# Tying the second block's preparation on VectorE to the place in the FFN where it was emitted

## The chip, the cores and the metric

The kernel runs on one core of a Trainium2 chip. The metric is the device time of one execution in microseconds. The kernel before takes 1735.87 us (median of 3 runs, 1732.74 to 1736.22).

## What is computed

A sequence of 512 tokens of width 1024 goes through two blocks. Block 1 is a gated delta rule beside a dilated attention, and then an FFN with a short convolution on its gate:

```python
h = rmsnorm(x, ln2[l])
gate = causal_dwconv(h @ w_gate[l], ffn_conv[l])
x = x + (jax.nn.silu(gate) * (h @ w_up[l])) @ w_down[l]
```

Block 2 mixes an SSM (`s5_mixer`) with a sparse attention and ends in a mixture of experts; an `ada` vector modulates it. Part of block 2 depends on weights alone. For the SSM that is the powers of each state's complex decay, the discretised input matrix, and tables of their products with the output matrix:

```python
mag = jnp.exp(lr * dt)
ab_re, ab_im = mag * jnp.cos(li * dt), mag * jnp.sin(li * dt)
bb_re = cr[..., None] * br - cim[..., None] * bim
```

For `ada` it is the product of a small vector `c` with a weight matrix of 1024 by 6144. This weight-only work is called the preparation here. The FFN's width is 2816, which is 22 column chunks of 128.

## The kernel before

`body` builds block 1, then hands the preparation to a `Filler` and calls `ffn`. The preparation is two generators run side by side by `both`, `ssm_prep` and `ada`; each `yield` ends a piece. `ffn` asks for pieces with `F.tick`: one before each gate load and one before each up load of a pair of chunks, two before each down load, and `F.finish()` for the rest in the last group.

`ffn` works in three groups of 8, 8 and 6 chunks. In a group, `K.ws` (L171 to L173) computes gate and up for a pair of chunks, c and c+1, in 48 matmuls each. `act` (L1013 to L1025) applies the convolution, the activation and the split into a high and a low part (`ahi`, `alo`). Then the down product (L1051 to L1053) runs in two halves of the output, n=0 and n=1, each over four weight tiles u=0, 2, 4, 6 of 24 matmuls. Every 128x1024 weight tile is loaded by SyncE (L143), rounded to `whi` on ScalarE (L153), and its remainder `wlo` is taken on VectorE (L154). TensorE uses a tile as three products, the third (second in the down product) with `wlo`. `wraw`, `whi` and `wlo` have three buffers each, the PSUM accumulators `mm` a ring of four.

The preparation's own parts that the text speaks of: on VectorE the `ada` accumulations L1117 and L1119, two of them after each load of an `araw` tile (L1111, two buffers) and 96 in all; chains of small 128x16 to 128x64 operations (L1204 to L1245), five doublings of a cosine and sine table (L1275 to L1280), and `bb` (L1317 to L1322). On GpSimd `pmul` (L1350 to L1352) builds V1 from `bb` in 48 operations, then the 16 tiles `s5v` (two buffers), which SyncE stores to `V3d` (L1368). `crow` are four loads (L1333) that TensorE transposes (L1335).

A tile scheduler orders each engine's instructions: it knows of data and buffers, not of the pieces' places. Nothing ties an instruction of a piece to the tick that emitted it, so it may be put ahead of FFN instructions that were emitted before it. An engine then runs its list in order.

Of the kernel before, what the change touches and what calls it, by code (L numbers as in the profile page):

```python
# [9 lines left out]
F32 = mybir.dt.float32  # L10
# [55 lines left out]
def both(a, b):  # L66
    for _ in zip_longest(a, b):
        yield


class Filler:


    def __init__(self):
        self.q = []

    def add(self, *gens):
        self.q.extend(gens)
# [1 line left out]
    def tick(self, n=1):  # L80
        while n and self.q:
            try:
                next(self.q[0])
                n -= 1
            except StopIteration:
                self.q.pop(0)
# [7 lines left out]
class Core:  # L94
# [54 lines left out]
    def split(self, raw, m=1024, eng=None, pool=None, bufs=3):  # L149

        nc = self.nc
        hi, lo = ((pool or self.w).tile([128, 1024], F32R, name=n, tag=n, bufs=bufs) for n in ("whi", "wlo"))
        nc.scalar.copy(hi[:, :m], raw[:, :m])  # L153
        (eng or nc.vector).tensor_sub(lo[:, :m], raw[:, :m], hi[:, :m].bitcast(F32))  # L154
        return hi, lo

    def ws(self, src, c0, n, xhi, xlo, nk, width=T):
# [202 lines left out]
def block1_mix(K):  # L360
# [3 lines left out]
    w_in = i["w_in"][0]  # L364
    F = Filler()
    left, right = ExitStack(), ExitStack()
# [32 lines left out]
    gst = ExitStack()  # L399
    G = Gdn(K, gst, F, w_in, hhi, hlo)  # L400
    G.first(wt)
# [9 lines left out]
    qk = S.qk_proj(0)  # L411
    F.add(qk)
    G.scan(yhi[0], ylo[0])
# [32 lines left out]

    F.finish(qk)
    S.attend(sst, F, out_half(0, False), yhi[1], ylo[1])
    F.add(out_half(1, True))
    F.finish()  # L450
# [525 lines left out]
def ffn(K, x, ss, F, last):  # L976


    nc, tc, i = K.nc, K.tc, K.i
    wg, wu, wd = i["w_gate"][0], i["w_up"][0], i["w_down"][0]  # L980
    with ExitStack() as st:
        P = lambda *a, **k: st.enter_context(K.pool(*a, **k))
        hp = P(name="fh", bufs=1)
        hhi = hp.tile([128, 8, T], F32R, name="hhi")
        hlo = hp.tile([128, 8, T], F32R, name="hlo")
        g = K.colvec(hp, i["ln2"][0], 8, "ln2c")
        wt = []
        with K.pool(name="fx", bufs=1, side="right") as xp:
            def rms(h):
                sq = K.col(2, "ss")  # L990
                nc.vector.tensor_add(sq, ss[:, 0, 2 * h:2 * h + 2], ss[:, 1, 2 * h:2 * h + 2])
                return K.rms(sq)

            xn = K.scale_half(0, x, rms(0), xp)
            wt += [K.wcol(wg, 0)]
            at = K.norm_half(0, xn, g, hhi, hlo, xp)
            xn = K.scale_half(1, x, rms(1), xp)
            with K.tc.issue_after(at.ins):
                wt += [K.wcol(w, c) for w, c in ((wg, 128), (wu, 0))]
            K.norm_half(1, xn, g, hhi, hlo, xp)  # L1000
        cw = hp.tile([128, 22, 3], F32, name="fcw")
        ps = K.aux()
        for j in range(3):
            rows = K.sm.tile([22, 128], F32, name="fcr", tag="cvrow", bufs=2)
            nc.scalar.dma_start(rows, i["ffn_conv"][0, j].rearrange("(k p) -> k p", p=128))
            nc.tensor.transpose(ps[:, 22 * j:22 * j + 22], rows, K.ident[:22, :22])
        nc.vector.tensor_copy(cw.rearrange("p c j -> p j c"), ps[:, :66].rearrange("p (j c) -> p j c", j=3))
        ap = P(name="fa", bufs=1)
        tp = P(name="ft", bufs=2)

        def act(c, gp, up):
            y = tp.tile([128, T], F32, name="fy", bufs=3)
            nc.scalar.activation(y, gp, AF.Copy, scale=cw[:, c, 2:3])  # L1013
            for j in range(2):
                s = 2 - j
                nc.vector.scalar_tensor_tensor(y[:, s:], gp[:, :T - s], cw[:, c, j:j + 1], y[:, s:],
                                               op0=OP.mult, op1=OP.add)
            th = tp.tile([128, T], F32, name="fth", bufs=3)
            nc.scalar.activation(th, y, AF.Tanh, scale=0.5)
            nc.vector.scalar_tensor_tensor(y, th, 1.0, y, op0=OP.add, op1=OP.mult)  # L1020
            nc.vector.scalar_tensor_tensor(th, y, 0.5, up, op0=OP.mult, op1=OP.mult)  # L1021
            hi = ap.tile([128, T], F32R, name="ahi", tag="ahi", bufs=9)
            lo = ap.tile([128, T], F32R, name="alo", tag="alo", bufs=9)
            nc.scalar.copy(hi, th)
            nc.vector.tensor_sub(lo, th, hi.bitcast(F32))  # L1025
            return hi, lo

        pre = {}
        K.ws_first(wt, hhi, hlo, pre.__setitem__)
        for _ in K.ws_pieces(wu, 128, 128, hhi, hlo, 8, lambda c, p: pre.__setitem__(3, p)):  # L1030
            pass
        c0 = 0
        for cn in (8, 8, 6):
            A = []
            for c in range(c0, c0 + cn, 2):
                if c:
                    F.tick(1)
                    gps = K.ws(wg, c * 128, 256, hhi, hlo, 8)
                    F.tick(1)
                    ups = K.ws(wu, c * 128, 256, hhi, hlo, 8)  # L1040
                else:
                    gps, ups = (pre[0], pre[1]), (pre[2], pre[3])
                for e in range(2):
                    A.append(act(c + e, gps[e], ups[e]))

            def product(ps, t, u, hi, lo):
                tt = slice(t * 128, (t + 1) * 128)
                for k in range(2):
                    kk = u + k
                    a, b = A[kk]  # L1050
                    nc.tensor.matmul(ps, a[:, tt], hi[:, k, :], start=kk == 0, stop=False)  # L1051
                    nc.tensor.matmul(ps, a[:, tt], lo[:, k, :], start=False, stop=False)
                    nc.tensor.matmul(ps, b[:, tt], hi[:, k, :], start=False, stop=kk == cn - 1)  # L1053

            def load(u, n):
                return K.wload(wd[(c0 + u) * 128:(c0 + u + 2) * 128, n * 512:(n + 1) * 512], 2, 512)

            def add(n, t, ps):
                o = x[:, t, n * 512:(n + 1) * 512]
                nc.vector.tensor_add(o, o, ps)  # L1060
                if end:
                    last(n, t)

            end = c0 + cn == FF // 128
            if end:
                F.finish()
                last(None, None)
            for n in range(2):
                if n and end:
                    wt = [load(u, n) for u in range(0, cn, 2)]  # L1070
                    for t in range(NT):
                        ps = K.mm()
                        for u in range(0, cn, 2):
                            product(ps, t, u, *wt[u // 2])
                        add(n, t, ps)
                else:
                    ps = [K.mm() for _ in range(NT)]
                    for u in range(0, cn, 2):
                        F.tick(2)
                        w = load(u, n)  # L1080
                        for t in range(NT):
                            product(ps[t], t, u, *w)
                    for t in range(NT):
                        add(n, t, ps[t])
            c0 += cn
# [1415 lines left out]
def body(tc, i, out):  # L2501
    with ExitStack() as ctx:
        K = Core(ctx, tc, i)
        x, ss = block1_mix(K)
        mats, mod = [], {}
        bst = ExitStack()
        bp = bst.enter_context(K.pool(name="bg", bufs=1, side="right"))
        F = Filler()
        F.add(both(ssm_prep(K, bp, mats), ada(K, bp, mod, K.keep)))
        B = Between(K, x, mod, bst)  # L2510
        ffn(K, x, ss, F, B)
        block2(K, x, B, mats, mod, out)
# [55 lines left out]
```

## Time and profile before

| | before |
|---|---|
| median of 3 runs | 1735.87 us |
| profiled execution | 1735.8 us |
| its span | 1734.0 us |
| mean granted TensorE clock | 0.973 |
| TensorE matmul, busy | 1616.4 us (93%) |
| VectorE, busy | 932.5 us (54%) |
| ScalarE, busy | 633.5 us (37%) |
| GpSimd, busy | 324.6 us (19%) |

The profile shows one execution, in us from its first instruction. TensorE is busy nearly throughout. Its busy share alone does not tell whether it runs at full speed: a matmul that runs at the lower of the two clocks counts as busy for longer.

### The profile page before, as it was taken

How to read it: one execution, taken by the hardware profiler on the slowest of the kernel's cores; microseconds unless marked ns; L12 is line 12 of the kernel's file. 1: busy time of each engine (PE TensorE's matmuls, PEld its weight loads, DVE VectorE, ACT ScalarE, POOL GpSimd, SP SyncE). 2: the span in 40 equal slices, each digit the busy share in tenths (PEclk: the TensorE clock that was granted, in tenths of full speed). 3: DMA queues.
4: the chain of work that ended last, by engine and by line, in shares of the span. 5: the costliest groups of instructions: out<-in, count | busy, mean ns of one | idle time of the engine just before them, and what ended most of it. 6: DMA issues, size and time to landing. Idle time of an engine off the chain costs nothing. (4 is left out here: it accounts for less than half of the span.)

```text
span 1734.0 us, 25313 instructions
## 1 busy us (share of the span) xinstructions
PE 1616.4 (93%) x9552; PEld 1177.0 (68%) x9552; DVE 932.5 (54%) x2106; ACT 633.5 (37%) x1280; POOL 324.6 (19%) x382
## 2 busy tenths in 40 slices
PE   7999999999889999999999999999999967999981
PEld 6777786678667888788877666666568745655540
DVE  6764276559988766555766544544434453221214
ACT  5534246444222432345343454545543320100001
POOL 1212110000809100003310221111211241111102
PEclk9999999999999999999999999999999987999996
DMA  5221131137277567327744112111117677999994
GB/s 156 58 68 56 44 110 65 46 111 208 73 237 232 177 201 216 104 79 203 184 115 146 43 43 62 49 44 49 43 62 245 226 284 282 418 418 418 418 401 173
DMA packets 173440, 284.73 MB, mean 164 GB/s; under 512 B 42754, under 2 KB 119557, under 8 KB 160645
## 3 DMA queue, kind: packets, MB, share of 16 engines
q1 hardware_dynamic: 167506, 273.07, 46.9%
q0 software_dynamic: 4896, 8.40, 1.3%
q8 instruction: 76, 1.25, 0.3%
q10 hardware_dynamic: 915, 1.64, 0.3%
q14 instruction: 47, 0.39, 0.1%
HBM read 262.07 MB, written 30.43 MB: 169 GB/s over the span
## 5 line engine op out<-in xcount | busy, mean ns | idle before, releaser
L154 DVE TENSOR_TENSOR wlo<-wraw,whi 128x1024 fp32r<-128x1024 f32 x162 | 207.1, 1280 | 143.2 <-ACT whi L153 140.5
L153 ACT CAST whi<-wraw 128x1024 fp32r<-128x1024 f32 x164 | 171.3, 1047 | 239.5 <-PE mm L1053 73.3
L213 PE MATMUL mm<-hhi,whi 128*128 128x512 f32 x440 | 186.4, 424 | 2.0 <-ACT whi L153 2.0
L215 PE MATMUL mm<-hhi,wlo 128*128 128x512 f32 x440 | 178.6, 407 | 0.1
L214 PE MATMUL mm<-hlo,whi 128*128 128x512 f32 x440 | 178.1, 405 | 0.0
L2274 PE MATMUL mm<-eraw,xt 128*64 128x256 f32 (+1 forms) x1024 | 129.4, 388 | 6.6 <-DMA eraw<-in_moe_w_up 4.8
L173 PE MATMUL mm<-hhi,wlo 128*128 128x512 f32 x320 | 127.5, 398 | 7.1 <-DVE wlo L154 7.1
L171 PE MATMUL mm<-hhi,whi 128*128 128x512 f32 x320 | 128.1, 400 | 0.0
L172 PE MATMUL mm<-hlo,whi 128*128 128x512 f32 x320 | 126.8, 396 | 0.0
L2274 PEld LDWEIGHTS mm<-eraw,xt 128*64 128x64 f32 (+1 forms) x1024 | 88.3, 141 | 44.2 <-DMA eraw<-in_moe_w_up 6.6
L213 PEld LDWEIGHTS mm<-hhi,whi 128*128 128x128 f32 x440 | 83.7, 190 | 25.7 <-issue 5.4
L215 PEld LDWEIGHTS mm<-hhi,wlo 128*128 128x128 f32 x440 | 83.6, 190 | 24.3 <-issue 5.3
L214 PEld LDWEIGHTS mm<-hlo,whi 128*128 128x128 f32 x440 | 84.0, 191 | 19.6 <-issue 5.6
L1745 DVE CUSTOM_DVE_ANT_0 NP<-mm,ncst 128x512 f32<-128x512 f32 (+3 forms) x128 | 61.5, 481 | 56.3 <-PE aux L1773 30.5
L1748 ACT ACTIVATE NP<-NP,mx 128x512 f32<-128x512 f32 (+3 forms) x128 | 72.1, 564 | 51.7 <-DVE mx L1745 51.3
L1753 POOL TENSOR_SCALAR NP<-NP,rden,gate 128x512 f32<-128x512 f32 (+3 forms) x64 | 40.2, 628 | 233.7 <-DVE rden L1750 196.7
L1119 DVE SCALAR_TENSOR_TENSOR acc<-araw,cs,acc 128x512 f32<-128x512 f32 x84 | 67.0, 798 | 19.8 <-DMA araw<-in_ada_w 18.4
L173 PEld LDWEIGHTS mm<-hhi,wlo 128*128 128x128 f32 x320 | 60.6, 189 | 22.6 <-DVE wlo L154 8.3
L1051 PE MATMUL mm<-whi,ahi 128*128 128x512 f32 x176 | 71.3, 406 | 4.3 <-DVE fth L1021 3.0
L171 PEld LDWEIGHTS mm<-hhi,whi 128*128 128x128 f32 x320 | 60.7, 190 | 15.0 <-issue 0.8
L172 PEld LDWEIGHTS mm<-hlo,whi 128*128 128x128 f32 x320 | 60.7, 190 | 13.9
L1053 PE MATMUL mm<-whi,alo 128*128 128x512 f32 x176 | 69.8, 397 | 0.0
(773 smaller groups left out, 3351.6 us busy)
## 6 DMA issues: line engine op xcount, KB each, us to landing
wraw<-in_w_in SPq DMA_DIRECT2D x68, 512.0 KB
eraw<-in_moe_w_gate SPq DMA_DIRECT2D x32, 1024.0 KB
eraw<-in_moe_w_up SPq DMA_DIRECT2D x32, 1024.0 KB
eraw<-in_moe_w_down SPq DMA_DIRECT2D x25, 1024.0 KB
araw<-in_ada_w SPq DMA_DIRECT2D x48, 512.0 KB
wraw<-in_w_gate SPq DMA_DIRECT2D x22, 512.0 KB
wraw<-in_w_up SPq DMA_DIRECT2D x22, 512.0 KB
wraw<-in_w_down SPq DMA_DIRECT2D x22, 512.0 KB
```

The lines of the kernel that those rows point to most:

```text
L153: nc.scalar.copy(hi[:, :m], raw[:, :m])
L154: (eng or nc.vector).tensor_sub(lo[:, :m], raw[:, :m], hi[:, :m].bitcast(F32))
L171: nc.tensor.matmul(o, hi[:, k, a:a + m], xhi[:, kk, :], start=kk == 0, stop=False)
L172: nc.tensor.matmul(o, hi[:, k, a:a + m], xlo[:, kk, :], start=False, stop=False)
L173: nc.tensor.matmul(o, lo[:, k, a:a + m], xhi[:, kk, :], start=False, stop=kk == nk - 1)
L213: nc.tensor.matmul(ps, hi, xhi[:, k, :], start=k == 0, stop=False)
L214: nc.tensor.matmul(ps, hi, xlo[:, k, :], start=False, stop=False)
L215: nc.tensor.matmul(ps, lo, xhi[:, k, :], start=False, stop=k == nk - 1)
L1051: nc.tensor.matmul(ps, a[:, tt], hi[:, k, :], start=kk == 0, stop=False)
L1053: nc.tensor.matmul(ps, b[:, tt], hi[:, k, :], start=False, stop=kk == cn - 1)
L1748: nc.scalar.activation(p[:, :n], p[:, :n], AF.Exp, scale=-1.0, bias=m, accum_out=d)
L2274: nc.tensor.matmul(ph[n][s], xt[:, k, s], r[n][:, k * 256:(k + 1) * 256], start=k == 0, stop=k == 7)
```

## The change

Each VectorE instruction of a piece gets an ordering edge behind one FFN instruction, the one that was VectorE's last in the FFN when the piece was emitted: the last `alo`, or, in the down loop and before `finish`, the last `wlo`. `tc.issue_after` sets that edge. No computation is added or taken away. On ScalarE two loads of an activation table are added, since the two sines of the preparation no longer stand side by side. After the end of the second group the orders of all engines are the same as before.

```diff
@@ class Filler
-    def __init__(self):
-        self.q = []
+    def __init__(self, tc=None):
+        self.q, self.tc, self.after = [], tc, None
@@ def tick
-                next(self.q[0])
+                with self.tc.issue_after(self.after) if self.after else ExitStack():
+                    next(self.q[0])
@@ def split
-        (eng or nc.vector).tensor_sub(lo[:, :m], raw[:, :m], hi[:, :m].bitcast(F32))
+        at = (eng or nc.vector).tensor_sub(lo[:, :m], raw[:, :m], hi[:, :m].bitcast(F32))
+        if not eng:
+            self.lo_at = at.ins
@@ ffn, act
-            nc.vector.tensor_sub(lo, th, hi.bitcast(F32))
+            F.after = nc.vector.tensor_sub(lo, th, hi.bitcast(F32)).ins
@@ ffn, last group
             if end:
+                F.after = K.lo_at
                 F.finish()
@@ ffn, down loop
                     for u in range(0, cn, 2):
+                        F.after = K.lo_at
                         F.tick(2)
@@ body
-        F = Filler()
+        F = Filler(tc)
```

Three places show what moves. In the changed kernel line numbers are larger by 1 from L144 on, by 3 to 5 in the preparation and the down product.

The first is VectorE ahead of `wlo_4843`, the second weight tile of the up product of c=6 (the first group). Before:

```order
L1275 TENSOR_TENSOR cm2_4924<-sinT_4326,ph0i_4899 128x16x16
L1279 TENSOR_TENSOR sinT_4326<-cosT_4325,ph0i_4899 128x16x16
L1277 TENSOR_TENSOR cosT_4325<-cosT_4325,cm2_4924 128x16x16
L1240 TENSOR_TENSOR cm1_4779<-ph0i_4899 128x16
L1244 TENSOR_TENSOR ph1i_4901<-ph0r_4898,ph0i_4899 128x16
L1278 TENSOR_TENSOR cm2_4924<-sinT_4326,ph0r_4898 128x16x16
L1242 TENSOR_TENSOR ph1r_4900<-ph1r_4900,cm1_4779 128x16
L1280 TENSOR_TENSOR sinT_4326<-sinT_4326,cm2_4924 128x16x16
L1243 TENSOR_TENSOR cm1_4779<-ph0i_4899,ph0r_4898 128x16
L1276 TENSOR_TENSOR cosT_4325<-cosT_4325,ph1r_4900 128x16x32
L154 TENSOR_TENSOR wlo_4843<-wraw_4840,whi_4842 128x1024
L1245 TENSOR_TENSOR ph1i_4901<-ph1i_4901,cm1_4779 128x16
```

And with the change:

```order
L1124 SCALAR_TENSOR_TENSOR acc_4416<-araw_4599,cs_4328,acc_4416 128x512
L1209 TENSOR_SCALAR nf_4519<-thh_4689 128x16
L1237 MEMSET aki_4774 128x16
L1239 TENSOR_TENSOR aki_4774<-mg_4513,thss_4595 128x16
L1210 CAST ni_4518<-nf_4519 128x16
L1122 TENSOR_SCALAR acc_4801<-araw_4802,cs_4328 128x512
L1211 CAST nf_4519<-ni_4518 128x16
L1245 TENSOR_TENSOR cm1_4779<-aki_4774 128x16
L1124 SCALAR_TENSOR_TENSOR acc_4801<-araw_4802,cs_4328,acc_4801 128x512
L1216 SCALAR_TENSOR_TENSOR thh_4689<-nf_4519,thh_4689 128x16 x3
L1217 TENSOR_SCALAR thh_4689<-thh_4689 128x16
L155 TENSOR_TENSOR wlo_4843<-wraw_4840,whi_4842 128x1024
```

Before, the fourth doubling of the cosine and sine tables and the start of the fifth and last (128x16x32) stand ahead of this tile. With the change the argument reduction of the second sine stands there, and no doubling stands ahead of the tile.

The second is VectorE ahead of `wlo_5169`, the tile u=6 of the first half (n=0) of the first group's down product. Before:

```order
L1119 SCALAR_TENSOR_TENSOR acc_5010<-araw_5015,cs_4328,acc_5010 128x512
L1021 SCALAR_TENSOR_TENSOR fth_4874<-fy_4870,mm_4808 128x512
L1119 SCALAR_TENSOR_TENSOR acc_5010<-araw_5061,cs_4328,acc_5010 128x512
L1025 TENSOR_TENSOR alo_4879<-fth_4874,ahi_4878 128x512
L1119 SCALAR_TENSOR_TENSOR acc_5010<-araw_5061,cs_4328,acc_5010 128x512
L1021 SCALAR_TENSOR_TENSOR fth_4886<-fy_4882,mm_4809 128x512
L154 TENSOR_TENSOR wlo_5082<-wraw_5079,whi_5081 128x1024
L1025 TENSOR_TENSOR alo_4891<-fth_4886,ahi_4890 128x512
L1119 SCALAR_TENSOR_TENSOR acc_5010<-araw_5077,cs_4328,acc_5010 128x512 x2
L154 TENSOR_TENSOR wlo_5169<-wraw_5166,whi_5168 128x1024
L1128 TENSOR_TENSOR modc_4336<-modc_4336,aux_5007 128x4
```

And with the change:

```order
L1307 TENSOR_TENSOR cr_5125<-cr_5125,den_5123 128x16
L1309 TENSOR_TENSOR ta_5127<-nr_5124,li_4414 128x16
L1122 TENSOR_SCALAR acc_5159<-araw_5160,cs_4328 128x512
L1310 TENSOR_TENSOR ci_5126<-ci_5126,ta_5127 128x16
L1323 TENSOR_TENSOR bb0_5144<-B0_5141,cr_5125 128x256
L1311 TENSOR_TENSOR ci_5126<-ci_5126,den_5123 128x16
L1326 TENSOR_TENSOR bb1_5148<-B1_5145,cr_5125 128x256
L1322 TENSOR_TENSOR tb_5149<-B1_5145,ci_5126 128x256
L1124 SCALAR_TENSOR_TENSOR acc_5159<-araw_5160,cs_4328,acc_5159 128x512
L1324 TENSOR_TENSOR bb0_5144<-bb0_5144,tb_5149 128x256
L155 TENSOR_TENSOR wlo_5169<-wraw_5166,whi_5168 128x1024
```

Before, two instructions of `ada` and one of the FFN stand between the tiles u=4 (`wlo_5082`) and u=6. With the change 94 stand between them: the doublings, R8, `den`, `cr`, `ci`, eight of `ada`, and `bb` but for its last two.

The third is SyncE's queue around the weight loads of c=8 and c=10 (`wraw_5561` and `wraw_5591` are the up tiles of c=8, `wraw_5669` the first gate tile of c=10). Before:

```order
L1111 DMA araw_5365<-in_ada_w_2 128x2x512
L143 DMA wraw_5515<-in_w_gate 128x4x256
L1111 DMA araw_5429<-in_ada_w_2 128x2x512
L1368 DMA V3d_4322<-s5v_5645 128x256
L1111 DMA araw_5433<-in_ada_w_2 128x2x512
L143 DMA wraw_5561<-in_w_up 128x4x256
L1111 DMA araw_5481<-in_ada_w_2 128x2x512
L1368 DMA V3d_4322<-s5v_5652 128x256
L1111 DMA araw_5557<-in_ada_w_2 128x2x512
L143 DMA wraw_5591<-in_w_up 128x4x256
L1368 DMA V3d_4322<-s5v_5729 128x256
```

And with the change:

```order
L144 DMA wraw_5561<-in_w_up 128x4x256
L1116 DMA araw_5365<-in_ada_w_2 128x2x512
L1116 DMA araw_5429<-in_ada_w_2 128x2x512
L144 DMA wraw_5591<-in_w_up 128x4x256
L1373 DMA V3d_4322<-s5v_5645 128x256
L1116 DMA araw_5433<-in_ada_w_2 128x2x512
L1116 DMA araw_5481<-in_ada_w_2 128x2x512
L1373 DMA V3d_4322<-s5v_5652 128x256
L144 DMA wraw_5669<-in_w_gate 128x4x256
L1373 DMA V3d_4322<-s5v_5729 128x256
L1116 DMA araw_5557<-in_ada_w_2 128x2x512
L1373 DMA V3d_4322<-s5v_5736 128x256
```

Before, the first store of `s5v` (`V3d`) stands ahead of both up tiles of c=8. With the change both stand ahead of it, the loads `araw_5433` and `araw_5481` follow right behind it, and the first gate tile of c=10 stands behind the second store instead of the fourth.

## Rows read from the trace of the kernel before

**Rows 1.** TensorE's waits, 399 to 700 us: what for, us, times, longest us.

```profile
PE mm L173 <- DVE wlo L154: 7.1, 2, 6.1
PE mm L1051 <- DVE fth L1021: 3.0, 2, 2.5
PE mm L1051 <- DVE fy L1016: 1.2, 1, 1.2
PE aux L1335 <- DMA crow<-in_ssm_c_im: 0.6, 1, 0.6
```

**Rows 2.** Busy time by stretch: length, PE, PEld, DVE, ACT, POOL (instructions), granted clock, DMA.

```profile
460.00:480.00 20.00, 13.85 (x52) 10.30 (x51) 19.97 (x47) 4.82 (x7) 13.03 (x18) 0.83 0.19 55
```

**Rows 3.** TensorE's timeline: start us, us, instruction [idle before it, what ended it].

```profile
451.01 0.50 PE L171 MATMUL mm<-hhi,whi 128*128 128x512 f32 x1
...
470.71 0.80 PE L173 MATMUL mm<-hhi,wlo 128*128 128x512 f32 x1 [6.08 <-DVE wlo L154]
471.30 0.63 PE L171 MATMUL mm<-hhi,whi 128*128 128x512 f32 x1
471.73 0.63 PE L172 MATMUL mm<-hlo,whi 128*128 128x512 f32 x1
...
483.14 0.39 PE L173 MATMUL mm<-hhi,wlo 128*128 128x512 f32 x1
483.38 0.40 PE L1051 MATMUL mm<-whi,ahi 128*128 128x512 f32 x1
...
537.88 0.40 PE L171 MATMUL mm<-hhi,whi 128*128 128x512 f32 x1
```

**Rows 4.** VectorE's timeline, in the first group: same columns.

```profile
440.06 0.66 DVE L1241 TENSOR_TENSOR ph1r<-ph0r 128x16 f32<-128x16 f32 x1
...
469.03 1.62 DVE L154 TENSOR_TENSOR wlo<-wraw,whi 128x1024 fp32r<-128x1024 f32 x1
...
475.22 0.17 DVE L1240 TENSOR_TENSOR cm<-ph0i 128x16 f32<-128x16 f32 x1
475.31 0.16 DVE L1244 TENSOR_TENSOR ph1i<-ph0r,ph0i 128x16 f32<-128x16 f32 x1
475.39 0.41 DVE L1278 TENSOR_TENSOR cm<-sinT,ph0r 128x256 f32<-128x256 f32 x1
...
478.21 0.69 DVE L1275 TENSOR_TENSOR cm<-sinT,ph1i 128x512 f32<-128x512 f32 x1
478.82 0.68 DVE L1279 TENSOR_TENSOR sinT<-cosT,ph1i 128x512 f32<-128x512 f32 x1
```

**Rows 5.** GpSimd while it builds V1, and while it builds `s5v`: length, busy (instructions), ...

```profile
436.87:473.10 36.23, 35.70 (x48) 0.92 0.19 55
521.35:567.20 45.85, 42.69 (x48) 1.00 0.72 223
```

**Rows 6.** VectorE by kind, 515 to 567 us: busy us, mean ns | idle before.

```profile
L1119 DVE SCALAR_TENSOR_TENSOR acc<-araw,cs,acc 128x512 f32<-128x512 f32 x19 | 18.3, 964 | 6.5 <-DMA araw<-in_ada_w 6.1
L1060 DVE TENSOR_TENSOR xres<-xres,mm 128x512 f32<-128x512 f32 x4 | 2.6, 674 | 0.0
```

**Rows 7.** The same, 570 to 700 us, where GpSimd is idle.

```profile
L154 DVE TENSOR_TENSOR wlo<-wraw,whi 128x1024 fp32r<-128x1024 f32 x22 | 26.9, 1221 | 22.3 <-ACT whi L153 22.3
L1119 DVE SCALAR_TENSOR_TENSOR acc<-araw,cs,acc 128x512 f32<-128x512 f32 x35 | 26.2, 750 | 8.2 <-DMA araw<-in_ada_w 7.6
L1060 DVE TENSOR_TENSOR xres<-xres,mm 128x512 f32<-128x512 f32 x8 | 5.5, 683 | 2.0 <-PE mm L1053 2.0
```

**Rows 8.** SyncE's queue: waits (515 to 570 us), and from its timeline two issues.

```profile
SPq L1368 <- POOL s5v L1352: 26.0, 15, 3.2
...
409.57 1.94 SPq L1111 DMA_DIRECT2D araw<-in_ada_w  x2
522.68 0.34 SPq L1368 DMA_DIRECT2D V3d<-s5v  x1
```

**Rows 9.** VectorE behind the first of those `araw` issues.

```profile
413.58 1.54 DVE L1119 SCALAR_TENSOR_TENSOR acc<-araw,cs,acc 128x512 f32<-128x512 f32 x2 [0.35 <-DMA araw<-in_ada_w]
```

## The prediction

> **What bounds the kernel now.** I read TensorE's waits first, because its busy share leaves little room elsewhere. Between 399 and 700 us they are few [rows 1]: 7.1 us for a `wlo` in the up product (two waits, of which one is 6.1), 3.0 + 1.2 us where the down product waits for VectorE's last reads of the up and gate accumulators, 0.6 us for a `crow` load. That is 11.9 us, all in the first group. The reader should then see in the busy times by stretch why: in 460 to 480 VectorE is busy 19.97 of 20.00 us while TensorE has 13.85 [rows 2]. The granted clock of that stretch is 0.83, so there is a second loss that no wait shows. In TensorE's timeline it stands right behind the 6.08 us of idleness: matmuls start 0.43 us apart (471.30, 471.73) instead of 0.24 (483.14, 483.38) [rows 3], so they run at 1.2 instead of 2.4 GHz. Eight matmuls run so here and about five after the wait of 2.5; at 0.2 us each that is 2.6. So the first group loses 11.9 + 2.6 = 14.5 us. It is the most that the change can give back there.
>
> Why is VectorE full? Its own timeline shows preparation around GpSimd's V1. A 128x16 operation takes 0.66 us there [rows 4] and 0.17 (0.09 from start to start) once V1 has ended; the `wlo` that TensorE waits for takes 1.62 against a mean of 1.22 [rows 4, 7]. GpSimd builds V1 from 436.87 to 473.10 [rows 5]. Hence the wait: VectorE runs the table doublings ahead of `wlo`, four times slower than alone.
>
> **The change part by part.** It adds no work on VectorE and makes the list in which that work stands later. The first place that the order shows is `wlo` in up of c=6: with the change no doubling stands ahead of it. There VectorE keeps up, and V1 can't have begun, since `bb` now comes in the down product. I take all of the 7.1 us and the 1.6 us behind it as gone. The waits on `fy` and `fth` (4.2 us) and 1.0 of half speed go as well, since these reads no longer stand behind 512-wide doublings. Removed: 14.5 with `crow`, which I let come back below.
>
> What comes instead, in order of time:
>
> In the second half of the norm eight steps of the reciprocal root (0.12 us each, from the small operations of [rows 4]) and one scaling of 1024 elements now stand ahead of the next two `wlo`, before only one step. The tiles come 1.0 and 1.7 us later. TensorE has 16 transposes moved up to fill some of it. I take +1.2, bounds 0.3 and 1.7.
>
> Then the down product. With the change it should start at 483.38 - 7.1 - 1.6 + 1.2, about 475.5 (gate of c=6 starts at 451.01 before [rows 3]). From 483.38 to 537.88 there are eight weight tiles in 54.5 us; less 4.8 of waits and 1.0 of half speed one tile takes 6.1. So tile u=6 is due at 475.5 + 3 x 6.1 = 493.8, and its `wlo` after four more matmuls, at 494.7. VectorE's list between the first `fth` of c=6 and this `wlo` has 114 instructions: 61 of 128x16 at 0.095 (5.8 us), 18 of 32 to 128 elements at some 0.14, between these (2.5), 10 of 256 at 0.33 (3.3), 6 of 512 at 0.61 and one of 1024 (4.2), 8 `ada` multiply-adds at 0.67 and two first ones at 0.4 (6.2), two `wlo` at 1.14 (2.3), four of the FFN's at 0.6 and two tiny ones (2.6). From start to start an operation costs its duration less 0.08 [rows 4, 7]. The sum is 26.9 us. The `fth` can start when its accumulator is complete, twelve matmuls before 475.5, so at about 473.1. `wlo` then begins at 500.0 and is there at 501.2: a wait of 6.5, and 1.6 of half speed behind it as after the 6.08. Bounds: 2, where VectorE starts some microseconds earlier on preparation that the order leaves free; 12, where the doublings meet V1 or wait for `araw`. The `crow` loads land about the same time and hide behind it: SyncE issues them behind the table's store, which waits for R8 in this same list.
>
> At the start of n=1 four `xres` additions and `nCT1` stand ahead of the next `wlo`. The last addition needs the last matmul of n=0; then 0.3, 0.7 and 1.3 us follow while TensorE has four matmuls (0.9) to do. I take +2.3 with `xres` itself, bounds 0 and 4.
>
> Last, V1 moves from 437 to about 500.5, beside n=1. The first `s5v` is then 51 GpSimd operations away. The nearest rows are 36.23 / 48 = 0.755 us each and 45.85 / 48 = 0.955 [rows 5], the second measured beside many `ada` multiply-adds. That puts its store between 539 and 549; I take 544 (before: 522.68 [rows 8]). SyncE's queue has `araw_5433` and `araw_5481` behind this store. A load lands 4.0 us after its issue (409.57 to 413.58) [rows 8, 9], and VectorE's list has the multiply-adds on both ahead of the last additions of n=1 and of the first `wlo` of up in c=8. Store and two issues 1.4, landing 4.0, one multiply-add and `wlo` 2.4: 7.8 us, so that `wlo` is there at 551.8. TensorE: n=0 ends at 507.5 with the losses above, n=1 at 507.5 + 2.3 + 24.4 = 534.2, gate of c=8 takes 11.4 (48 matmuls at 0.237), and `wlo` is due at 546.0. Wait 6, bounds 0 (store before 538) and 11, with half speed 1.6 behind it.
>
> The page "SBUF — State Buffer" of the Trainium skill, section "Who interferes with whom", bears on this term: VectorE and GpSimd share one lock, and a VectorE operation that reads two SBUF inputs keeps out a GpSimd operation that reads SBUF, and the other way round, while one that reads PSUM does not. The trace agrees in kind. Beside GpSimd the `ada` multiply-add takes 964 ns against 750 alone [rows 6, 7], the `xres` addition from PSUM 674 against 683. Taken strictly, each GpSimd operation beside a multiply-add would cost both durations; the row of 0.955 is less than that.
>
> Sum: 1.2 + 6.5 + 1.6 + 2.3 + 6 + 1.6 = 19.2 in place of 14.5, so +4.7 on the profiled 1735.8 us, or about 1740.5. The median of the runs, 1735.87, is the same within 0.1, so I use it as it stands. Three runs span 3.5 us (0.2%); a change under 0.2% can't be told from none.
>
> **Rivals.** *VectorE keeps up.* If more of the list between the tiles is done early and the store comes before 538, only 1.2 + 2.3 are left, and the time is 1735.8 - 14.5 + 3.5, about 1725. For it: until 500 no VectorE operation runs beside V1, so everything before runs at its price alone. Against it: the order puts 94 instructions between two tiles, which no wait can move.
>
> *The down product waits, c=8 does not.* V1 at 0.755 or less and stores in time: 1.2 + 6.5 + 1.6 + 2.3 = 11.6, about 1733, no change that can be told. For it: VectorE waits for `araw` and leaves GpSimd alone at times. Against it: [rows 5], second row, is the kind of VectorE work that stands beside V1 now.
>
> *Strict alternation.* GpSimd's operation waits out a whole multiply-add: 0.62 + 0.75 = 1.37 us while VectorE is busy (some 20 operations until 530), then 0.62 for 31 more. The store comes at about 549 to 551, the wait is 11 to 13, the time about 1746.
>
> *The stores block the weights (slower).* SyncE already waits 26.0 us in 15 times for `s5v` [rows 8], and nobody pays, since the weights behind are early. With the first store some 21 us later, weight loads of c=10 and c=12 stand behind stores in the queue. Each pair of stores takes 4.5 to 5.7 us (six GpSimd operations), a weight product of two tiles 11.4. From a first store at about 549 on, the loads come after the product needs them, and TensorE waits for `whi` itself: another 12 us, about 1752.
>
> *The change does nothing.* The order excludes it: VectorE's list differs over the whole first group.
>
> **How the numbers follow.** The forecast, 1735 to 1747 by its own bounds, 0.43; VectorE keeps up 0.17; down waits alone 0.20; strict alternation 0.08; stores block weights 0.12. Outside 1726 to 1751 I leave a little of the first and the last. Slower: 0.12 + 0.08 + most of the forecast (0.28) = 0.48. Faster: 0.17 + a part of the third (0.08) = 0.25. The rest, 0.27, is no change: 0.12 of the third and 0.15 of the forecast.
>
> **What would show it.** In the profile after: no wait on `wlo` between 440 and 475 and a start of down near 475.5, else the first step is wrong. One wait of 4 to 8 us on `wlo` at about 495 to 501, matmuls 0.43 us apart behind it. Small VectorE operations at 0.17 us there, since V1 has not begun; V1 from about 500 on, at 0.75 to 0.96 us an operation. The first store at 539 to 549, and a wait in up of c=8 on `wlo` or an accumulator. If TensorE waits there for `whi`, the stores have taken the weights' place in the queue. If no wait over 2 us is left, VectorE kept up and I was wrong in the count of what must run between two tiles.

## The result and the profile after

The changed kernel takes 1746.08 us (median of 5 runs, 1743.82 to 1748.70), the kernel before 1736.22 beside it: a ratio of 1.0061, 95% interval 1.0040 to 1.0081. One of the five runs of the kernel before took 1830.85 us and is left out of the ratio. The changed kernel is slower by 9.9 us; 4.7 had been forecast. Its profiled execution took 1748.7 us, span 1746.9, and is the longest of the five: 12.9 more than the profiled run of before, of which 2.2 lie in block 1, ahead of the change.

TensorE's waits after, from 370 to 720 us (what for, us in total, times, longest; three small ones, 2.1 us together, are not shown), answer to [rows 1]:

```profile
PE mm L174 <- DVE xres L1063: 5.1, 1, 5.1
PE mm L1055 <- DVE wlo L155: 4.5, 2, 2.9
PE aux L1340 <- DMA crow<-in_ssm_c_im: 4.4, 2, 3.9
PE aux L1127 <- DVE acc L1124: 3.6, 3, 2.0
PE mm L176 <- DVE wlo L155: 2.5, 1, 2.5
PE mm L304 <- DVE hlo L333: 1.6, 2, 1.1
```

No old wait is left but `crow`. Of the new ones the 1.6 us on `hlo`, and 0.7 of those not shown, lie in the norm ahead of gate and up; the others are later in the program than those of before. The busy times by stretch (length, PE, PEld, DVE, ACT, POOL, clock, DMA) say it again:

```profile
440.00:460.00 20.00, 20.00 (x94) 15.82 (x93) 13.47 (x28) 8.60 (x13) 0.00 (x0) 1.00 0.42 131
460.00:480.00 20.00, 20.00 (x89) 16.20 (x88) 17.88 (x59) 10.36 (x13) 0.00 (x0) 1.00 0.63 183
...
500.00:520.00 20.00, 14.14 (x45) 10.53 (x46) 18.84 (x28) 1.05 (x1) 17.15 (x18) 0.74 0.63 209
...
540.00:560.00 20.00, 12.60 (x51) 9.33 (x50) 5.00 (x6) 2.80 (x3) 19.70 (x30) 0.87 0.38 112
```

460 to 480, the worst stretch of before [rows 2], is full now and at full clock. In 500 to 520 TensorE has lost 5.9 us and a quarter of its clock while VectorE is busy for 18.84 of 20.00. In 540 to 560 it has lost 7.4 while VectorE is three quarters idle.

The matmul starts in the two timelines split the difference by stage:

| from the start of ... | before | after | difference | forecast |
|---|---|---|---|---|
| program to the last matmul of block 1 | 375.5 | 377.7 | +2.2 | 0 |
| that to the first group's down product | 107.8 | 99.8 | -8.1 | -7.5 |
| down product to gate of c=8 | 54.5 | 62.6 | +8.1 | +4.6 |
| gate of c=8 to the second down product | 90.6 | 103.6 | +13.0 | +7.6 |
| second down product to the third group | 52.6 | 54.3 | +1.7 | 0 |
| third group to the FFN's last matmul | 103.4 | 103.2 | -0.2 | 0 |
| that to the end of the span | 949.6 | 945.8 | -3.8 | 0 |

The second row hides two opposite differences. From the last matmul of block 1 to the first 128x512 matmul of gate or up, which is the norm with the narrower products in it, TensorE takes 25.8 us instead of 23.9; from there to the down product it takes 74.0 instead of 84.0.

The FFN alone is slower by 14.5 us; the last row gives 3.8 back. In the ten profiles of this study, whose work after the FFN is the same, that row lies between 945.8 and 950.0. The kernels with the latest FFN have short ones (945.8 and 946.6), but one whose FFN ended only 2.0 us later than before has 946.3. Whether it is a return or differs from run to run was not settled.

**The first new wait** is in n=0 at tile u=6. TensorE's timeline (start, us, instruction, in brackets the idle time before and its end):

```profile
496.33 0.52 PE L1340 MATMUL aux<-ident,crow 128*128 128x128 f32 x2
500.76 0.45 PE L1340 MATMUL aux<-ident,crow 128*128 128x128 f32 x1 [3.91 <-DMA crow<-in_ssm_c_im]
501.73 0.45 PE L1340 MATMUL aux<-ident,crow 128*128 128x128 f32 x1 [0.53 <-DMA crow<-in_ssm_c_im]
503.81 0.80 PE L1055 MATMUL mm<-wlo,ahi 128*128 128x512 f32 x1 [1.63 <-DVE wlo L155]
504.40 0.63 PE L1056 MATMUL mm<-whi,alo 128*128 128x512 f32 x1
504.82 0.63 PE L1054 MATMUL mm<-whi,ahi 128*128 128x512 f32 x1
```

6.07 us of waiting, divided between the `crow` loads and a `wlo` that is there 2.1 us behind the last of them, and then matmuls 0.42 apart, that is 1.2 GHz, as after the 6.08 of [rows 3]. VectorE's timeline at the end of its list:

```profile
501.51 0.77 DVE L1124 SCALAR_TENSOR_TENSOR acc<-araw,cs,acc 128x512 f32<-128x512 f32 x1
502.17 0.44 DVE L1324 TENSOR_TENSOR bb<-bb,tb 128x256 f32<-128x256 f32 x1
502.51 1.25 DVE L155 TENSOR_TENSOR wlo<-wraw,whi 128x1024 fp32r<-128x1024 f32 x1
503.64 0.44 DVE L1325 TENSOR_TENSOR tb<-B,ci 128x256 f32<-128x256 f32 x1
```

No bracket stands in it: the engine goes from one instruction to the next, and `wlo` is simply the 95th behind the tile u=4.

**The second** is at c=8. GpSimd's timeline gives V1's start and the first `s5v`, SyncE's the store and the loads behind it, VectorE's what waits for them:

```profile
502.70 1.86 POOL L1355 TENSOR_TENSOR s5t<-bb,akr 128x256 f32<-128x256 f32 x1 [9.68 <-DVE bb L1324]
...
549.13 0.73 POOL L1357 TENSOR_TENSOR s5v<-s5t 128x256 f32<-128x256 f32 x1
```

```profile
530.72 0.37 SPq L144 DMA_DIRECT2D wraw<-in_w_up  x1
549.89 0.34 SPq L1373 DMA_DIRECT2D V3d<-s5v  x1
550.32 0.93 SPq L1116 DMA_DIRECT2D araw<-in_ada_w  x2
```

```profile
537.50 1.27 DVE L1063 TENSOR_TENSOR xres<-xres,mm 128x512 f32<-128x512 f32 x2
555.00 0.75 DVE L1124 SCALAR_TENSOR_TENSOR acc<-araw,cs,acc 128x512 f32<-128x512 f32 x1 [16.23 <-DMA araw<-in_ada_w]
555.66 0.68 DVE L1063 TENSOR_TENSOR xres<-xres,mm 128x512 f32<-128x512 f32 x1
556.26 1.09 DVE L1124 SCALAR_TENSOR_TENSOR acc<-araw,cs,acc 128x512 f32<-128x512 f32 x1
557.27 0.68 DVE L1063 TENSOR_TENSOR xres<-xres,mm 128x512 f32<-128x512 f32 x1
557.87 0.74 DVE L1124 SCALAR_TENSOR_TENSOR acc<-araw,cs,acc 128x512 f32<-128x512 f32 x1
558.53 1.64 DVE L155 TENSOR_TENSOR wlo<-wraw,whi 128x1024 fp32r<-128x1024 f32 x1
```

SyncE issues nothing for 19 us, since the store at the head of its queue waits for GpSimd. So `araw`, which waits for nothing itself, comes late; VectorE stands 16.23 us in front of a multiply-add that nobody needs yet; the addition behind it, which frees TensorE's accumulator, is late:

```profile
556.49 0.77 PE L174 MATMUL mm<-hhi,whi 128*128 128x512 f32 x1 [5.08 <-DVE xres L1063]
...
560.22 0.79 PE L176 MATMUL mm<-hhi,wlo 128*128 128x512 f32 x1 [2.54 <-DVE wlo L155]
```

### The profile page after: what moved, and what is told of

It is laid out like the page before. It is cut to its first block, busy times and chain, and to the rows that moved or that the text cites. A ratio compares the mean times of both kernels' runs of the same rounds, so it can differ in the third digit from the quotient of the medians.

```text
span 1746.9 us, 25312 instructions
## 1 busy us (share of the span) xinstructions
PE 1616.4 (93%) x9552; PEld 1176.6 (67%) x9552; DVE 920.0 (53%) x2106; ACT 637.2 (36%) x1282; POOL 325.3 (19%) x382
## 5 line engine op out<-in xcount | busy, mean ns | idle before, releaser
L216 PEld LDWEIGHTS mm<-hhi,whi 128*128 128x128 f32 x440 | 83.6, 190 | 25.8 <-issue 5.4
L218 PEld LDWEIGHTS mm<-hhi,wlo 128*128 128x128 f32 x440 | 83.2, 189 | 24.4 <-issue 5.3
L1055 PE MATMUL mm<-wlo,ahi 128*128 128x512 f32 x176 | 71.0, 404 | 4.5 <-DVE wlo L155 4.5
```

The source lines that it names most:

```text
L216: nc.tensor.matmul(ps, hi, xhi[:, k, :], start=k == 0, stop=False)
L218: nc.tensor.matmul(ps, lo, xhi[:, k, :], start=False, stop=k == nk - 1)
```

## The experiments

The theory after the result: the gain is what was taken from beside V1; the loss is made of two things, 94 instructions that must run between two weight tiles, and a late V1, whose first store stands in SyncE's queue ahead of loads that others need. Rivals: V1 beside VectorE costs TensorE the same wherever it runs; or whatever is tied costs. Ratios are to the kernel before, run beside each on the same chip (medians 1734 to 1735 us).

**The store out of SyncE's queue.**

```diff
-            nc.sync.dma_start(V3d[r, :, t], v)
+            nc.gpsimd.dma_start(V3d[r, :, t], v)
```

> The changed kernel with one edit: the 16 stores of s5v to V3d are issued by GpSimd itself and no longer stand in SyncE's queue; VectorE's order is that of the changed kernel, word for word. Theory (the late store holds SyncE's queue): the two araw loads come before the additions of n=1 need them, VectorE's idle stretch of 16.2 us at 539 to 555 goes, and with it TensorE's 5.1 us on xres and 2.5 us on wlo in c=8, the 2.0 us on acc at 580 and some 2.5 us of half speed: 1732 to 1738 us. Rival (contention with V1 alone makes c=8 late): VectorE's operations stay as slow as they are beside GpSimd, a wait of 4 us or more stays at c=8, at least 1742 us.

1741.9 us, ratio 1.0047 (1.0030 to 1.0065), which is between the two ranges, and its interval overlaps that of the changed kernel: the median alone does not show a gain. The trace shows the step itself as expected: neither `xres` nor `wlo` is waited for at c=8, and that stage takes 93.1 us instead of 103.6.

```profile
PE mm L1055 <- DVE wlo L155: 5.5, 2, 2.8
PE aux L1127 <- DVE acc L1124: 4.1, 2, 2.1
PE aux L1340 <- DMA crow<-in_ssm_c_im: 3.5, 2, 3.1
```

The wait on `acc` behind it did not go, as had been expected: 2.1 us instead of 2.0. And the down product ahead of it takes 66.0 us instead of 62.6: more matmuls run at half speed (27 in place of 12), and a wait on `acc` in n=1 is 2.0 instead of 1.3. Most of this loss can't come from the edit. SyncE issues the same loads in the same order in both up to 532.5 us, and its first load that the store had held back goes out at 535.27, just as that wait ends and when 21 of the 27 have run. So the queue makes the waits of 7.6 us at c=8, and the stage got 10.5 shorter; why the half speed lasts longer ahead of it, in a single profile, was not settled.

**Only `bb` tied, on the kernel before.** The six `bb` instructions are put behind the last `wlo`; all else is free.

```diff
+    with K.tc.issue_after(K.lo_at):
         nc.vector.tensor_mul(tb, Bm[1], bh(ci))
         nc.vector.tensor_mul(bb[0], Bm[0], bh(cr))
...
         nc.vector.tensor_add(bb[1], bb[1], tb)
```

> The kernel before with one edit: only the six VectorE instructions that make bb are tied behind the last wlo at the place where they are emitted (the down product of the first group); all other preparation is as free as before. So V1 can't start before about 490, while the doublings stay early. Theory (V1 beside VectorE made the 14.5 us of before; the list of 94 between two tiles made the wait in n=0 of after): no wait over 1 us on wlo, fy or fth between 440 and 500, no wait on wlo at u=6, but the first store as late as 535 to 548 and a wait of 3 to 9 us at c=8, as after has: 1727 to 1736 us. Rival (the amount of preparation ahead of wlo, not its price beside V1, made the wait of 6.1): a wait of 4 us or more on wlo in up of c=6 stays, 1738 us or more.

1738.3 us, ratio 1.0021 (1.0007 to 1.0035), somewhat above the theory's range and by its time just inside the rival's; the waits decide, 370 to 720 us:

```profile
PE mm L173 <- DVE xres L1062: 17.4, 1, 17.4
PE aux L1338 <- DMA crow<-in_ssm_c_im: 2.0, 1, 2.0
PE mm L302 <- ACT whi L153: 0.2, 1, 0.2
```

The wait on `wlo` of 4 us or more that the rival asks for is not there. With V1 away from gate and up, all waits of [rows 1] on VectorE are gone, though the doublings are as early and as many as before: their price beside V1 made those waits, not their number. With the doublings early, nothing waits at u=6. The doublings also run at their price alone: the five are done at 460 us, and gate and up take 74.1 us.

What remains is one wait of 17.4 us, far more than the 3 to 9 expected. SyncE's queue and VectorE's timeline show it:

```profile
502.32 0.37 SPq L1113 DMA_DIRECT2D araw<-in_ada_w  x1
523.26 0.34 SPq L1371 DMA_DIRECT2D V3d<-s5v  x1
```

```profile
528.93 1.78 DVE L1121 SCALAR_TENSOR_TENSOR acc<-araw,cs,acc 128x512 f32<-128x512 f32 x2 [20.34 <-DMA araw<-in_ada_w]
```

The store was expected at 535 to 548 and came at 523.3, hardly later than before (522.68 [rows 8]), since V1 began at 477.0. It is late only for its place in the queue: TensorE reaches the down product at 471.7, before at 483.4, and needs what is queued behind the store that much earlier.

**Both edits together.**

> The edit of e2_bb_tied and that of e1_store_own_queue together on the kernel before. Theory: neither the waits of before nor that at c=8 are left; waits between 399 and 700 sum to under 4 us, 1718 to 1726 us, the fastest of all. Rival (V1 beside VectorE costs TensorE the same wherever it runs): about 7 us of waits in n=1 and c=8, 1730 us or more.

1720.9 us, ratio 0.9924 (0.9905 to 0.9943), the fastest kernel of the study: 13 us below the one before, and by the two ratios some 24 below the changed one.

```profile
PE mm L173 <- DVE xres L1062: 1.5, 1, 1.5
PE aux L1338 <- DMA crow<-in_ssm_c_im: 1.3, 1, 1.3
```

V1 runs beside VectorE here too, in the down product, and TensorE loses nothing by it there (length, PE, PEld, DVE, ACT, POOL, clock, DMA):

```profile
480.00:500.00 20.00, 20.00 (x96) 15.92 (x97) 17.59 (x21) 4.10 (x6) 19.75 (x21) 1.00 0.68 202
```

Its waits from 399 to 720 us sum to 2.8. That ends the rival by which the contention costs the same wherever it is. No matmul of the FFN runs at half speed.

**The queue alone, on the kernel before**, the missing corner of the square.

> The kernel before with the stores of s5v issued by GpSimd instead of SyncE, and nothing else. It is the missing corner of a square: before, stores alone, bb alone (e2_bb_tied), both (e3_bb_tied_own_queue). Theory (the two edits need each other: with V1 early the stores hold up nobody): the waits of 7.1, 3.0 and 1.2 us in the first group stay, 1732 to 1738 us, no change. Rival (the queue alone gives what e3 gains): 1724 us or less.

1732.6 us, ratio 0.9995 (0.9983 to 1.0007): no change, and the waits stand as in [rows 1].

```profile
PE mm L173 <- DVE wlo L154: 6.5, 2, 6.0
PE mm L1051 <- DVE fth L1021: 3.2, 2, 2.5
```

So neither edit gains alone: the one moves V1, and only then does the other take a wait away.

**The ties ahead of gate and up alone, stores on SyncE.**

```diff
-                        F.after = K.lo_at
+                        F.after = None
                         F.tick(2)
```

(and none before `finish`)

> The changed kernel without the ties in the down product and at the end: pieces emitted ahead of gate and up loads stay tied, pieces emitted in the down product are free. The order still has some 75 preparation instructions between the tiles u=4 and u=6 of n=0, since the doublings wait for the tied pieces ahead of them. Theory: the wait at u=6 stays at 4 to 8 us and that at c=8 too, 1739 to 1748 us. Rival (the ties in the down product make the loss): 1735 us or less.

1743.6 us, ratio 1.0053 (1.0033 to 1.0073), as the theory has it. At u=6 TensorE waits 2.4 + 0.6 + 2.9 us, at c=8 0.9 + 3.5. The ties in the down product do little: once the first pieces are held back, the doublings behind them come late by their data.

**`crow` out of SyncE's queue**, on the first experiment's kernel.

```diff
-                nc.sync.dma_start(rw[:, par * 64:par * 64 + 64],
+                nc.scalar.dma_start(rw[:, par * 64:par * 64 + 64],
```

> The kernel of e1_store_own_queue with the crow loads moved from SyncE's queue to ScalarE's, so that they no longer stand behind the table's store and the stores of s5z. VectorE's order in the down product is the same. Theory (the list of 94 on VectorE sets the wait at u=6): the wait on crow (3.5 us) goes and the one on wlo grows by as much, 6 to 7 us in all; 1740 to 1744 us, as e1. Rival (the queue order of SyncE sets it): the waits at u=6 fall to about 2.7 us, 1737 to 1739 us.

1739.2 us, ratio 1.0022 (1.0008 to 1.0036), between the two ranges expected, so that the time does not decide. The waits at u=6 are 2.9 + 1.4 on `crow` and 1.8 on `wlo`, 6.2 as without the edit, and end with `wlo`:

```profile
496.22 0.45 PE L1340 MATMUL aux<-ident,crow 128*128 128x128 f32 x1 [2.92 <-DMA crow<-in_ssm_c_im]
498.08 0.45 PE L1340 MATMUL aux<-ident,crow 128*128 128x128 f32 x1 [1.42 <-DMA crow<-in_ssm_c_im]
500.35 0.79 PE L1055 MATMUL mm<-wlo,ahi 128*128 128x512 f32 x1 [1.82 <-DVE wlo L155]
```

The `crow` loads stayed late on the other queue too, so this did not take that cost away. It speaks against SyncE's queue as the cause, but whether `crow` on time would shorten the wait was not shown by removal; that `wlo` ends it is. The median lies 2.7 us below the first experiment's, with overlapping intervals; their FFNs take the same (415.4 and 415.3 us from block 1's last matmul).

**The same pieces, spread earlier**, on the first experiment's kernel: two pieces ahead of each gate and up load of the first group, one ahead of each tile of n=0.

```diff
-                    F.tick(1)
+                    F.tick(2 if c < 8 else 1)
                     gps = K.ws(wg, c * 128, 256, hhi, hlo, 8)
...
-                        F.tick(2)
+                        F.tick(2 if c0 or n else 1)
```

> The kernel of e1_store_own_queue with the pieces placed earlier in the first group: two instead of one ahead of each gate and up load, one instead of two ahead of each tile of n=0. In the order the longest run of other instructions on VectorE between two wlo is then 62 (nearly all small), between the two tiles of up in c=6, and 21 or fewer between the tiles of n=0. Theory (the number of instructions between two tiles sets the wait): none at u=6, at most 3 us in up of c=6, bb some 15 us earlier, so that n=1 and c=8 go free as well: 1726 to 1734 us. Rival (what is tied at all costs, wherever it is): 1738 us or more.

1730.3 us, ratio 0.9978 (0.9965 to 0.9992). With every tie in place no `wlo` is waited for in the first group. What is left is for the most part new (the waits in the norm are as in the changed kernel and not shown):

```profile
PE aux L1127 <- DVE acc L1124: 10.0, 4, 3.4
PE mm L174 <- DVE xres L1063: 1.6, 1, 1.6
```

At 8 us below the rival's 1738 this ends the rival by which whatever is tied costs. TensorE also takes part in the preparation: it sums `ada`'s accumulators (L1127) in its own order and waits there when VectorE is late.

**The ties in the down product alone**, stores on GpSimd's queue: `F.after` stays empty ahead of gate and up.

> The kernel of e1_store_own_queue without the ties ahead of gate and up loads: only pieces emitted in the down product are tied. The order has 75 instructions between u=4 and u=6 instead of 94, and ada's first operations are back beside the norm. Theory: the 2.6 us of waits in the norm and its transposes go, the wait at u=6 shrinks by about 2 us: 1735 to 1739 us. Rival (the ties in gate and up cost nothing): 1741 to 1743 us as e1.

1732.0 us, ratio 0.9979 (0.9965 to 0.9993), better than expected. Little of the gain over the first experiment is in the norm, which takes 25.6 us instead of 26.1 (one wait of 1.2 us stayed). The down product takes 59.9 us instead of 66.0:

```profile
PE mm L1056 <- DVE wlo L155: 3.9, 2, 2.8
PE aux L1341 <- DMA crow<-in_ssm_c_im: 3.0, 1, 3.0
PE aux L1133 <- ACT acc L1130: 1.5, 2, 0.9
```

No wait on VectorE's `acc` is left: with `ada`'s first pieces free, its accumulators are done when TensorE comes to them. So the ties ahead of gate and up cost more than the theory gave them, part of it through `ada`, part at u=6 (4.1 for 6.2).

## Why the prediction was right, and where its sizes were off

- *The waits of before go.* Right: up to the down product the time is 8.1 us shorter, 7.5 forecast. Two errors of size cancel in it: gate and up gained 9.9 where 8.7 was taken, and the norm cost 1.9 where 1.2 was taken, outside its bounds of 0.3 and 1.7. That V1's price was the cause was argued then; the `bb` run shows it.
- *The wait at u=6.* Right: 6.07 for 6.5, six matmuls at half speed behind it. The list of 114 took 26.3 us (476.25 to 502.51), 26.9 forecast. `wlo` began at 502.5 for 500.0; since TensorE arrived 2 us later as well (block 1's share), the wait came out the same. The `crow` loads did not hide behind it: 4.4 of the 6.07 are put down to them, but the wait ends with `wlo`.
- *The start of n=1.* 2.85 us for 2.3, and six more matmuls at half speed, which had no term.
- *c=8.* The right mechanism, place and order of causes: V1 began at 502.7 (500.5 forecast), the first store came at 549.9 (544, bounds 539 to 549, so just outside). The term that was mis-sized is this one: 7.6 us in the sum, 13.0 in the trace. The waits of 5.08 and 2.54 are 7.6 where 6 was taken, inside its bounds. About 2.2 us of half speed came for 1.6, 0.6 of start-up between the two waits, and 2.0 of a wait on `acc` that had no term. TensorE met the late queue twice, first at the accumulator and then at `wlo`. From the store's issue to the end of that `wlo` 10.3 us passed where 7.8 had been counted: VectorE had three multiply-adds and two additions ahead of it, where one multiply-add had been counted. Against this TensorE itself came 5.9 us later than forecast (gate of c=8 at 540.1 for 534.2).
- *What had no term:* `ada`'s accumulators, 3.6 us of waits on `acc` in three places (1.6 of it in n=1, 2.0 at c=10), and 1.2 in the second down product. The sum had counted `ada`'s instructions on VectorE but not TensorE's reading of them.
- *GpSimd's pace.* 0.755 to 0.955 an operation had been the bounds. From 502.70 to 549.86 there were 54 operations in 47.2 us, 0.87 each: between the bounds, as taken. Three of them, two copies and an operation of the next tile, had not been counted; they and the later start make some 5 of the 6 us between forecast and store.

The sum has two slips: 483.38 - 7.1 - 1.6 + 1.2 is 475.9, not 475.5, and 475.5 + 24.4 + 6.5 + 1.6 is 508.0, not 507.5. Neither moves a wait by more than 0.5 us.

That the time still fell between 1735 and 1747 is in part luck. The bounds of the terms added up reach from about 1725 to 1753. The FFN of the profiled run lost 14.5 us, three times the forecast: 5.4 more than the sum had from c=8 to the second down product, 3.5 more in the first down product, 1.7 in the second. With nothing else changed this would have been 1750. The 3.8 us that came back behind the FFN had no term, and the median lies 0.9 us below the upper end.

Of the rivals, the strict alternation named the measured time (1746), but its way was not the one observed. By its own figures, 500.5 + 20 x 1.37 + 31 x 0.62, the store comes at 547.1, not at 549 to 551. It needed 1.37 us for each GpSimd operation beside VectorE; there were 32 in 32.32 us while VectorE was busy (505.63 to 537.95), 1.01 each. *VectorE keeps up* failed where it was said to, between the two tiles. Stores that block the weights themselves, for TensorE to wait on `whi`, did not occur.

## What to carry to other kernels

Before tying filler work to a place, count for each engine what must then run between two deadlines, and who else, a queue or another engine, takes what it makes. A store in a shared queue that waits for a slow engine turns that engine's lateness into everybody's; put it on the queue of the engine that it waits for. Where cheap work is dear beside something, move that one thing: here six tied instructions, with the stores on their own queue, gained 13 us, where tying all of them lost 10.

## What the runs showed of the hardware

- GpSimd and VectorE slow each other, and both lose. A GpSimd operation on 128x256 took 1.01 us beside a busy VectorE (505.63 to 537.95 of after) and 0.63 while VectorE stood idle (19 from 537.95 to 549.83). A VectorE multiply-add of 128x512 beside V1 took 1060 ns on the mean (14 of them, 503 to 537 us of after) against 750 alone [rows 7], a `wlo` 1633 against 1221, while the additions from PSUM took 681 against 683:

```profile
L1124 DVE SCALAR_TENSOR_TENSOR acc<-araw,cs,acc 128x512 f32<-128x512 f32 x14 | 14.8, 1060 | 2.3 <-DMA araw<-in_ada_w 2.1
L155 DVE TENSOR_TENSOR wlo<-wraw,whi 128x1024 fp32r<-128x1024 f32 x7 | 11.4, 1633 | 0.0
L1063 DVE TENSOR_TENSOR xres<-xres,mm 128x512 f32<-128x512 f32 x4 | 2.7, 681 | 1.2 <-PE mm L1056 1.2
```

- In these runs the number of matmuls at 1.2 GHz does not follow the length of the wait ahead of them. Behind the first matmul there are six after 2.85 us at 514 and six after 6.07 at 504 of after, 13 after 6.18 in the first experiment, and 12 after the 17.4 of the `bb` run.
- Block 1, which no kernel changed, ended between 373.3 and 377.7 us in these profiles. Stages of two single profiles are compared from their own starts, not from the program's.
